# WKV-7 recurrence: all four head pairs in one step, a written order on all compute engines, a triangular inverse by blocks of 16

## The chip, the cores and the metric

The kernel runs on one core of a Trainium2 chip. A core has TensorE (PE in the views; PEld is its weight load), VectorE (DVE), ScalarE (ACT), GpSimd (POOL) and SyncE (SP, which issues DMAs here). Each engine works through its own queue in order; semaphores tie the queues together. The metric is the device time of one execution in microseconds, as the median of several runs.

## The reference

One layer of a hybrid encoder block on 1024 positions with a model width of 1024, all in float32. After a norm and one input projection, branch A is latent attention with 8 heads, branch B the bidirectional WKV-7 recurrence with 8 heads of 64, and both are gated, merged and added to the input. A gated feed-forward part with a depthwise convolution follows.

```python
h = rms_norm(x)
proj = h @ w_in
o_a = mla_branch(...)                  # 8 heads, softmax over all positions
o_b = rwkv7_branch(...)                # see below
y = sig(gA) * (o_a @ w_o[:512]) + sig(gB) * (o_b @ w_o[512:])
x = x + y @ w_merge
x = x + (silu(dwconv(rms_norm(x) @ w_gate)) * (rms_norm(x) @ w_up)) @ w_down

def step(state, inp):                  # one position of one head, 64 x 64 state
    r_t, w_t, k_t, v_t, a_t, b_t = inp
    sa = einsum('bhvk,bhk->bhv', state, a_t)
    state = state * w_t + sa[..., None] * b_t + v_t[..., None] * k_t
    return state, einsum('bhvk,bhk->bhv', state, r_t)
# run once forward and once backward; then a norm per head, a bonus term and a gate
```

## The kernel before

**Stages.** Up to about 340 us the kernel projects the columns of both branches (`weave`). From there to about 1278 us runs a mixed stage, which the change rebuilds. Branch B's output product and the merge follow, to 1390 us, and then the feed-forward part with blocked products (L1591, L1684 to L1686), to the end. The change leaves the feed-forward part as it is.

**The dense stream of the mixed stage.** `dense()` hands out products in small pieces: `gates()` (16 tiles of gate columns, L254, L255, L257), `attention()` (8 heads of 16 steps) and `branch0()` (branch A's output product). A precise product is three matmuls: high part by high part, low by high and high by low; `split` makes the two parts with a cast on ACT (L168, `whi` from the loaded weights `wraw`) and a subtraction on POOL or DVE (L169, `wlo`). An attention step is three score matmuls (L1214 to L1216), the exponential on ACT (L123), a cast (`ph`, L1225), its low part (`pl`, L1226, POOL) and three products with the values (L1188 to L1190). `maxima` (L1158 to L1165) finds each row's largest score ahead of a head.

**The recurrence.** It is worked in chunks of 64 positions. A unit is one head pair and one half of the sequence, in both directions, 8 chunks; there are 8 units. `prep_a` makes for a unit the matrix `NM` (L798) and the inverse of each chunk's triangular 64 x 64 matrix: the two 32 x 32 blocks on its diagonal go through memory (`dn`, read back as `IN`) into a layout with one block a partition, and DVE eliminates them in 31 steps of a multiplication into `tm` (L819) and an addition into `Ti` (L823). The result goes through memory again in two layouts (`dT`, `dU`, read back as `TT` and `U`, L841 and L843), and two sets of matmuls (L852, L863) fill in the block beside the diagonal. `prep_b` makes the operands `Er` (L904), `Ek` (L915) and `BT` (L928).

**The chain.** `chain` then takes a unit's chunks one after the other. A chunk has three hops that wait for each other: L980 (the state `RR` times `Ek`, copied to `rh` on ACT), L992 (times the inverse `TT`, copied to `RR` by DVE and ACT, L993 and L994) and L1005 (times `BT`; on DVE, L1010, the product `sm` of the old state with the chunk's decay, which POOL has made at L988, is added). L952 sets the values into the next `RR`, and `chunk_out` (L961, L966) makes the output, which `gnorm` (L1034, L1044) normalises and gates. Each matmul set of a hop is four matmuls: two directions, two heads.

**What sets the order.** In the mixed stage only TensorE's instructions stand in the order in which the program writes them; DVE, ACT and POOL are ordered by a scheduler. The program writes them with a planner: its loop keeps a clock `now`, advances it by each dense piece, and emits a hop when the table `LATENCY` says that its inputs are there, a preparation step (`prepare`) when it is due, and else a dense piece (`fill`). `DENSE` is the dense work between two hops. In the feed-forward part all engines and SP stand in written order.

Of the kernel before, what the change touches and what calls it, by code (L numbers as in the profile page):

```python
# [25 lines left out]
NPAIR = 4  # L26
DECAY = math.exp(-0.5)
# [19 lines left out]
LAG = 3  # L47

LATENCY = {
    "a0": 4000, "a1": 5000, "a2": 4000, "a3": 4000, "nm": 2100, "nz": 7020, "inv": 32000, "u": 10000, "y": 2125, "t": 2500,  # L50
    "b0": 5600, "b1": 0, "b2": 3720, "er": 2400, "ak": 2160, "sb": 4900, "bt": 1500, "hop": 1000, "gn": 4500, "last": 1500,
}
AHEAD = 6
DENSE = (920, 1000, 1000, 1150, 1070, 1150, 1150, 1150)
CARRY = 1000
# [10 lines left out]
HOPC = 450  # L66
PREPC = 0.8
# [20 lines left out]
def block_kernel(ctx: ExitStack, tc: tile.TileContext, a):  # L88
    nc = tc.nc
    V, S, G = nc.vector, nc.scalar, nc.gpsimd  # L90
# [16 lines left out]
    cur = {"set": None, "load": None, "group": []}  # L107

# [37 lines left out]
    def dt(name, shape):  # L146
# [4 lines left out]
    d_rw = {q: [dt(f"d_{q}{p}", [128, T]) for p in range(NPAIR)]  # L151
            for q in ("r", "v", "kk", "x1", "x2", "s0", "s1", "bo")}
# [8 lines left out]
    d_oa, d_ob = ([[dt(f"d_o{b}{x}{p}", [128, T]) for x in "hl"] for p in range(NPAIR)] for b in "ab")  # L161
# [217 lines left out]

    def inproj(j, done):  # L380
        ps = big()
        for k in range(8):
            if k % 4 == 0:
                wh, wl = wcols(a["w_in"][j], k // 4)
            ws = slice(k % 4 * 128, (k % 4 + 1) * 128)
            mmk(ps, wh[:, ws], wl[:, ws], hx[k], k == 0, k == 7)
            if k == 7:
                done(ps)
            yield 1280
# [27 lines left out]

    now = [0.0]
# [153 lines left out]
    def rw_done(p, q):  # L572
        def done(ps):
            t = keep(q, "rkv"[q] + "t")
            shift(ps, 4 + 4 * q + p, t)
            if q != 1:
                nc.sync.dma_start(d_rw["rkv"[q]][p], t)
            rkv[p, q] = t
        return done

    def rw_prep(p):
# [4 lines left out]
        for dst, wt, src, bias, key in (  # L586
# [11 lines left out]
            if key:  # L598
                nc.sync.dma_start(d_rw[key][p], dst)
# [8 lines left out]
        for h in range(2):  # L608
            nc.sync.dma_start(d_rw[("x2", "x1")[h]][p][H[h], :], kf[H[h], :])
# [7 lines left out]
        nc.sync.dma_start(d_rw["kk"][p], nr)  # L617
        V.scalar_tensor_tensor(out=at, in0=at, scalar=-1.0, in1=nr, op0=mult, op1=mult)
        for h in range(2):
            nc.sync.dma_start(d_rw[("x1", "x2")[h]][p][H[h], :], at[H[h], :])  # L620
# [12 lines left out]
        nc.sync.dma_start(d_rw["bo"][p], bo)  # L633

    def gate_done(j):
        def done(ps):
            for x, hs in zip(ps, HT):
                gt = wpool["g"].tile([128, 512], F32, tag="gt", name="gt")
                V.tensor_tensor(out=gt, in0=x, in1=rstd[:, hs], op=mult)
                (S if j >= 14 else nc.sync).dma_start(d_gate[j][:, hs], gt)  # L640
# [56 lines left out]
    for p in range(NPAIR):  # L697
        weave(*[inproj(T_RKV + 3 * p + q, rw_done(p, q)) for q in (1, 0, 2)])
    parts(True)
# [5 lines left out]
    G.memset(smask.rearrange("p (c t) -> p c t", t=C)[:, :, 0:1], 0.0)  # L705
    TTt = [cbp.tile([128, NCH, C], F32, name=f"TT{d}") for d in range(2)]
# [3 lines left out]

    wpool["g"] = ctx.enter_context(pool("gp", side="right"))
    sb = ExitStack()
# [6 lines left out]

    def scb():  # L720
        return pw.tile([128, 512], F32, tag="sc", name="sc", bufs=SC_BUFS)

    def ctb():
        return pw.tile([128, 2, C], F32, tag="ct", name="ct", bufs=CT_BUFS)
# [7 lines left out]

    def half(src):
        t = wk.tile([128, 512], F32, tag="ld", name="ld", bufs=4)
        nc.sync.dma_start(t, src)
# [3 lines left out]
    def dirs(d, t):  # L739
        return (t if d == 0 else t[:, ::-1]).rearrange("p (f c t) -> p f c t", c=4, t=C)  # L740
# [4 lines left out]
    def after(key, i):  # L745

        if key in state:
            tc.add_manual_dep(i.ins, state[key].ins.name, NOSYNC, reason="after the recurrence's step")

    def prep_a(p, w, n, q):  # L750

        hts = (HT[w], HT[1 - w])
# [5 lines left out]
        sg = [half(d_rw[f"s{d}"][p][:, hts[d]]) for d in range(2)]  # L758
        x1 = [half(d_rw["x1"][p][:, hts[d]]) for d in range(2)]
        yield "a0", 0  # L760

        for d in range(2):
            t = sg[d] if d == 0 else sg[d][:, ::-1]
            after("dve", V.tensor_tensor_scan(t, smask, t, 0.0, mult, add))
            after("act", act(of(d, pin), dirs(d, sg[d]), AF.Exp, scale=-DECAY))
            act(of(d, iP), dirs(d, sg[d]), AF.Exp, scale=DECAY)
        pcs = wk.tile([128, NCH], F32, tag="pcs", name="pcs", bufs=3)
        wk.tile([128, 16], F32, tag="pad2", name="pad")
        V.tensor_copy(pcs[:, :, None], last)
        q.update(pin=pin, pcs=pcs)  # L770
        kk = [half(d_rw["kk"][p][:, hts[d]]) for d in range(2)]
        yield "a1", 0

        BK = [wk.tile([128, 8, 128], F32, tag="BK", name="BK", bufs=3) for _ in range(2)]
        AXk = [wk.tile([128, 8, C], F32, tag="AXk", name="AXk", bufs=3) for _ in range(2)]

        def times(eng, key, dst, src, f, cs):
            for hf in range(2):
                for d in range(2):
                    after(key, eng.tensor_tensor(out=dst[hf][:, 4 * d:4 * d + 4, cs], in0=dirs(d, src[d])[:, hf],  # L780
                                                 in1=of(d, f)[:, hf], op=mult))

        times(G, "pool", BK, x1, iP, H[0])
        times(V, "dve", AXk, kk, pex, H[0])
        x2 = [half(d_rw["x2"][p][:, hts[d]]) for d in range(2)]
        q.update(BK=BK, AXk=AXk)
        yield "a2", 0

        times(G, "pool", BK, x2, iP, H[1])
        yield "a3", 0  # L790

        NM = take("NM", n, [128, NCH, C])
        for c0_ in (0, 8):
# [6 lines left out]
            if c0_ == 0:  # L800
                yield "nm", 1300
        dn = dr.tile([2, 2, NCH, 32, 32], F32, tag="dn", name="dn", bufs=2)
        for h in range(2):
            for b in range(2):
                r0 = h * 64 + b * 32
                nc.sync.dma_start(dn[h, b].rearrange("c s t -> s c t"), NM[r0:r0 + 32, :, b * 32:b * 32 + 32])
        IN = take("IN", n, [128, 32, 32])
        for i in range(4):
            nc.sync.dma_start(IN[32 * i:32 * i + 32], dn[i // 2, i % 2][None].to_broadcast([2, NCH, 32, 32]))
        yield "nz", 1300  # L810

        Ti = wk.tile([128, 32, 16], F32, tag="Ti", name="Ti")
        G.memset(Ti, 0.0)
        for i in range(2):
            V.tensor_copy(Ti.rearrange("p t j -> p (t j)")[:, 16 * i:16 * i + 496:33], cst[:, C_TI + i:C_TI + i + 1].to_broadcast([128, 16]))
        for s in range(31):
            nt, nj = 31 - s, s // 2 + 1
            tm = wk.tile([128, 32, 16], F32, tag="tm", name="tm")
            t = V.tensor_tensor(out=tm[:, 0:nt, 0:nj], in0=IN[:, s, s + 1:32][:, :, None].to_broadcast([128, nt, nj]),  # L819
                            in1=Ti[:, s, 0:nj][:, None, :].to_broadcast([128, nt, nj]), op=mult)  # L820
            if s == 0:
                after("dve", t)
            V.tensor_tensor(out=Ti[:, s + 1:32, 0:nj], in0=Ti[:, s + 1:32, 0:nj], in1=tm[:, 0:nt, 0:nj], op=add)  # L823
        Tq = wk.tile([128, 16, 32], F32, tag="tm", name="Tq")
        S.copy(Tq, Ti.rearrange("p t j -> p j t"))
        dT = dr.tile([2, 2, 16, 2 * NCH, 32], F32, tag="dT", name="dT", bufs=2)
        dU = dr.tile([2, 32, 2 * NCH, 16], F32, tag="dU", name="dU", bufs=2)
        for h in range(2):
# [1184 lines left out]
```

## Time and profile before

| what | us |
|---|---|
| median of 3 runs (2094.4 to 2099.11) | 2096.95 |
| the profiled execution | 2094.12 |
| its span, by the profile | 2092.3 |

A row of a window gives, for a stretch from A to B, its length and each engine's busy time with the number of its instructions, then the clock that TensorE was granted as a share of full speed, the DMA engines' busy share and the bytes moved a second. A row of waits names the waiting engine, the tile and line it waits in, then what ended the wait, with the total, the number and the longest in us. A row of instructions by line gives busy time and the mean of one in ns, and behind the next bar the idle time ahead of them with what ended it. An fp32 matmul is worked in two passes and leaves two records.

### The profile page before, as it was taken

To read this page: it belongs to the slowest core of one execution; us is meant where nothing else is said; L and a number is where in the kernel's file an instruction comes from. 1 tells how busy PE (TensorE), PEld (TensorE's weight loads), DVE (VectorE), ACT (ScalarE), POOL (GpSimd) and SP (SyncE) were. 2 spreads that over 40 slices of the span, in tenths; PEclk is the share of its full clock that TensorE was granted. 3 is DMA by queue.
4 is the path that set the end of the run, shared out by engine and by line. 5 is a ranking of instruction groups with operands and counts; after the bars stand their busy time and mean duration, and the time that the engine had idled before them with its cause. 6 is when DMAs were issued, how large, how long until landed. Compare 5 with 4: busy or idle time off the path is not lost.

```text
span 2092.3 us, 31850 instructions
## 1 busy us (share of the span) xinstructions
PE 1900.7 (91%) x12016; PEld 1462.3 (70%) x12016; DVE 1316.8 (63%) x2112; ACT 912.6 (44%) x1603; POOL 821.1 (39%) x718
## 2 busy tenths in 40 slices
PE   7799999799898887788788999998999999999998
PEld 5566667676666565566556677876788888888887
DVE  7566666636383957585957134458767666766677
ACT  4676564123233454565556753444233233322331
POOL 7344546232223565555546632223522222222221
PEclk9999999899999888998989999999999999999999
DMA  3147446452436153434433378210111111111112
GB/s 146 34 142 229 141 163 205 124 142 75 137 95 174 43 141 99 94 99 114 108 88 94 102 272 298 94 57 30 51 61 46 61 46 61 46 61 45 61 47 100
DMA packets 216714, 221.09 MB, mean 106 GB/s; under 512 B 113960, under 2 KB 145768, under 8 KB 216560
## 3 DMA queue, kind: packets, MB, share of 16 engines
q1 hardware_dynamic: 215984, 218.01, 34.5%
q8 instruction: 94, 1.54, 0.3%
q10 hardware_dynamic: 576, 1.05, 0.1%
q14 instruction: 60, 0.49, 0.1%
HBM read 151.20 MB, written 63.60 MB: 103 GB/s over the span
## 4 chain that ended last, share of the span: by engine, by line
PE 44%; DVE 11%; DMA 4%; issue 2%; ACT 1%; SPq 1%; POOL 0%; DVEq 0%; ACTq 0%; POOLq 0%
PE b L1591 18%; PE b L1685 4%; PE b L1686 3%; PE b L1684 3%; DMA IN<-dn 2%; DVE Ti L823 2%; PE b L257 2%; PE b L254 2%; PE b L255 2%; DVE tm L819 2%; DVE mx L1159 1%; PE po L1188 1%; PE st L1214 1%; PE st L1215 1%; PE st L1216 1%
## 5 line engine op out<-in xcount | busy, mean ns | idle before, releaser
L169 POOL TENSOR_TENSOR wlo<-wraw,whi 128x512 fp32r<-128x512 f32 x118 | 161.8, 1372 | 512.3 <-ACT whi L168 506.6
L1226 POOL TENSOR_TENSOR pl<-pe,ph 128x512 fp32r<-128x512 f32 x128 | 169.8, 1329 | 131.5 <-ACT ph L1225 129.1
L254 PE MATMUL st<-hh,whi 128*128 128x512 f32 x408 | 176.4, 432 | 16.7 <-ACT hh L281 9.0
L255 PE MATMUL st<-hl,whi 128*128 128x512 f32 x408 | 165.2, 405 | 0.5 <-DVE hl L282 0.5
L1696 DVE TENSOR_TENSOR x<-b,x 128x512 f32<-128x512 f32 x176 | 119.2, 687 | 54.7 <-PE b L1686 54.7
L819 DVE TENSOR_TENSOR tm<-IN,Ti 128x126 f32<-128x126 f32 (+22 forms) x248 | 95.1, 383 | 80.2 <-DMA IN<-dn 74.0
L257 PE MATMUL st<-hh,wlo 128*128 128x512 f32 x408 | 141.5, 402 | 1.3 <-POOL wlo L169 1.3
L168 ACT CAST whi<-wraw 128x512 fp32r<-128x512 f32 x118 | 72.9, 619 | 142.2 <-PE po L255 35.2
L254 PEld LDWEIGHTS st<-hh,whi 128*128 128x128 f32 x408 | 79.8, 196 | 46.2 <-issue 11.1
L1225 ACT CAST ph<-pe 128x512 fp32r<-128x512 f32 x128 | 79.1, 620 | 65.3 <-PE po L1190 63.3
L823 DVE TENSOR_TENSOR Ti<-Ti,tm 128x126 f32<-128x126 f32 (+22 forms) x248 | 101.0, 407 | 6.6
L988 POOL TENSOR_TENSOR sm<-RR,pcs 64x128 f32<-64x128 f32 x112 | 47.5, 424 | 145.0 <-DVE RR L1010 108.6
L169 POOL TENSOR_TENSOR wl<-wraw,wh 128x512 fp32r<-128x512 f32 x22 | 28.9, 1313 | 179.7 <-ACT wh L168 179.7
L123 ACT ACTIVATE pe<-st 128x512 f32<-128x512 f32 x128 | 76.3, 597 | 39.9 <-PE st L1216 33.3
L257 PEld LDWEIGHTS st<-hh,wlo 128*128 128x128 f32 x408 | 79.3, 195 | 20.2 <-POOL wlo L169 2.2
L255 PEld LDWEIGHTS st<-hl,whi 128*128 128x128 f32 x408 | 80.0, 196 | 16.4 <-issue 1.2
L1159 DVE TENSOR_REDUCE mx<-st 128x1 f32<-128x512 f32 x112 | 73.3, 683 | 28.3 <-PE st L1158 28.0
L954 ACT COPY RR<-sc 64x256 f32<-64x256 f32 x128 | 47.0, 367 | 57.6 <-PE sc L952 53.2
L1684 PE MATMUL b<-sh,wh 128*128 128x512 f32 x176 | 69.1, 393 | 2.7 <-ACT sh L1640 2.7
L1685 PE MATMUL b<-sl,wh 128*128 128x512 f32 x176 | 69.3, 394 | 0.8 <-DVE sl L1649 0.8
L1684 PE MATMUL b<-sh,whi 128*128 128x512 f32 x176 | 68.6, 390 | 1.3 <-DVE x L1696 1.3
L1686 PE MATMUL b<-sh,wl 128*128 128x512 f32 x176 | 69.2, 393 | 0.0
(502 smaller groups left out, 5529.3 us busy)
## 6 DMA issues: line engine op xcount, KB each, us to landing
wraw<-w_in SPq DMA_DIRECT2D x64, 256.0 KB
wraw<-w_fd SPq DMA_DIRECT2D x44, 256.0 KB
AA<-w_fu SPq DMA_DIRECT2D x41, 256.0 KB
A<-w_fg SPq DMA_DIRECT2D x41, 256.0 KB
ld<-d_x SPq DMA_DIRECT2D x32, 256.0 KB
d_gate<-gt SPq DMA_DIRECT2D x28, 256.0 KB
xt<-xT SPq DMA_DIRECT2D x8, 512.0 KB
d_s<-sg SPq DMA_DIRECT2D x8, 512.0 KB
```

Source lines behind the costliest of these rows:

```text
L169: (eng or G).tensor_tensor(out=lo, in0=x, in1=hi.bitcast(F32), op=sub)
L254: nc.tensor.matmul(o, wh, xh[:, hs], start=first, stop=False)
L255: nc.tensor.matmul(o, wh, xl[:, hs], start=False, stop=False)
L257: nc.tensor.matmul(o, wl, xh[:, hs], start=False, stop=last)
L819: t = V.tensor_tensor(out=tm[:, 0:nt, 0:nj], in0=IN[:, s, s + 1:32][:, :, None].to_broadcast([128, nt, nj]), in1=Ti[:, s, 0:nj][:, None, : ...
L823: V.tensor_tensor(out=Ti[:, s + 1:32, 0:nj], in0=Ti[:, s + 1:32, 0:nj], in1=tm[:, 0:nt, 0:nj], op=add)
L1226: G.tensor_tensor(out=pl, in0=pe, in1=ph.bitcast(F32), op=sub)
L1591: nc.tensor.matmul(b, wt[:, ws], x, start=(first and k == 0 and m == 0), stop=(k == 3 and m == 2), skip_group_check=True)
L1684: nc.tensor.matmul(b, wh[:, ws], xh[:, hs], start=(k == 0), stop=False)
L1685: nc.tensor.matmul(b, wh[:, ws], xl[:, hs], start=False, stop=False)
L1686: nc.tensor.matmul(b, wl[:, ws], xh[:, hs], start=False, stop=(k == 1))
L1696: V.tensor_tensor(out=x2[j][:, hs], in0=b, in1=x2[j][:, hs], op=add)
```

## The change

The diff has 1303 lines. A unit is now 128 positions in each direction of all four head pairs: 8 units of 2 chunks. So `chain(n, q, osb)` has 16 steps instead of 64, and each matmul set runs over `EACH`, 8 slots of direction and pair, for two heads: 16 matmuls, with one evacuation. `RR` is two tiles, one for each head of a pair. The product with the decay moves from the operands and from `sm` onto the state itself: an addition on DVE and then a multiplication with `pcs` on POOL for one head and on DVE for the other.

The inverse is worked in blocks of 16: DVE eliminates in 15 steps, and the blocks beside the diagonal are filled in by matmuls in two levels, with products `P`, `X`, `PY`, `Y` and `TT`. `NM`'s blocks go to memory in 8 writes and return in one read; the inverse goes out in two writes and returns in 14 reads of 16 x 16 blocks (`Un` and `TT`).

DVE, ACT and POOL stand in written order in the mixed stage too. `Clocked` wraps each engine and keeps a planned clock of it, from a fixed cost and one for each element; the planner's loop reads these clocks instead of `LATENCY`. Rows of instructions that go through it name its line, L104. The four banks of PSUM with the tag `sc` are shared by the chain, the preparation and the maxima.

In attention every other step makes two exponentials on ACT (`ph` and, in place, the full value) and its low part on DVE; the other steps do as before. Weights of the gates and of branch A are loaded ahead through a queue (`queue`, `prefetch`, `weights`). `gnorm` works in pieces of 128 columns and keeps three of the four pairs' results in SBUF instead of writing them to memory. After the mixed stage the first two tiles of branch B's product are interleaved (`mixture`), and `x2` is loaded behind all of them.

```diff
-LAG = 3
-LATENCY = {
-    "a0": 4000, "a1": 5000, "a2": 4000, "a3": 4000, "nm": 2100, "nz": 7020, "inv": 32000, "u": 10000, "y": 2125, "t": 2500,
...
+LAG = 4
+DENSE = (1500,) * 8
+SLACK = 1500
+MARGIN = 300
+BACKLOG = 4000
+HOP = 300
+CARRY = 3000
...
+    V, S, G = Clocked(nc.vector, 140, 1.04), Clocked(nc.scalar, 140, 0.92), Clocked(nc.gpsimd, 100, 2.35)
...
+    written.enter_context(tc.manual_schedule(engines={getattr(mybir.EngineType, n) for n in ("PE", "DVE", "Activation", "Pool")}))
+    ordered(True)
...
-        for s in range(31):
-            nt, nj = 31 - s, s // 2 + 1
+        for s in range(15):
+            nt, nj = 15 - s, s + 1
...
+        for g in range(8):
+            rows, b = slice(16 * g, 16 * g + 16), g % 4
+            if b != 3:
+                nc.sync.dma_start(Un[rows, :, b % 2 * 16:b % 2 * 16 + 16], dU[g].rearrange("c t j -> t c j"))
+            nc.sync.dma_start(TT[rows, :, b * 16:b * 16 + 16], dT[g].rearrange("c j t -> j c t"))
...
+        for c, r, b in each4:
+            nc.tensor.matmul(p3[r:r + 32, c], NM[r:r + 16, c, b:b + 32], Un[r:r + 16, c, 0:16], start=True, stop=True)
+        S.activation(P, p3, AF.Copy, scale=cst[:, C_TI + 1:C_TI + 2])
...
-            for d in range(2):
+            for s, d, c in EACH:
                 for h, hs in enumerate(H):
-                    nc.tensor.matmul(ct[hs, d, :], BT[:, d, i % 4, hs], RR[:, d, h, 1, :], start=(d == 0), stop=(d == 1))
+                    nc.tensor.matmul(ct[hs, s, :], BT[:, d, c, hs], RR[h][:, s, 1, :], start=(s == 0), stop=(s == 7))
             for h, hs in enumerate(H):
...
-                    V.tensor_tensor(out=nxt[hs, :, h, 0, :], in0=ct[hs], in1=sm[hs], op=add)
+                    V.tensor_tensor(out=z, in0=ct[hs], in1=RR[h][hs, :, 0, :], op=add)
+                    (G if h == 0 else V).tensor_tensor(out=z, in0=z, in1=pc, op=mult)
...
-        for k in range(26):
+        for k in range(9):
...
-            now += HOPC
-            ready = now + LATENCY["hop"]
+            now[0] += x
+            ready = max(now[0], ends[0] + x) + HOP
```

The first place is in attention, on TensorE, around hops of the chain. Of before, with `st` the scores, `po` the products with the values and `ct` the chain's:

```order
L980 MATMUL ct<-RR,Ek 64x64 x4
L961 MATMUL ct<-Er,RR 64x64 x4
L966 MATMUL ct<-AXr_2707,RR 64x64 x4
L1214 MATMUL st<-qh_2721,kh_2722 128x512
L1215 MATMUL st<-ql,kh_2722 128x512
L1216 MATMUL st<-qh_2721,kl 128x512
L1158 MATMUL st<-kh_5988,qh_5987 128x512 x2
L992 MATMUL ct<-rh,TT_2691 64x64 x4
L952 MATMUL sc<-cst,vv 64x64 x4
L1188 MATMUL po<-ph,vhh_5989 128x512
```

Of the changed kernel at a like place (L1289 to L1291 are the scores, L1247 to L1249 the products with the values, L1217 the maxima, L858 the preparation's `NM`, L1055 the hop with the inverse):

```order
L858 MATMUL sc<-AXk,BK 64x64 x16
L1247 MATMUL po<-ph,vhh_6917 128x512
L1248 MATMUL po<-pl,vhh_6917 128x512
L1249 MATMUL po<-ph,vhl_6919 128x512
L1289 MATMUL st<-qh_2701,kh_2702 128x512
L1290 MATMUL st<-ql,kh_2702 128x512
L1291 MATMUL st<-qh_2701,kl 128x512
L1217 MATMUL sc<-kh_6915,qh_6914 128x512 x2
L1055 MATMUL ct<-rh,TT_2671 64x64 x16
L1247 MATMUL po<-ph,vhh_6916 128x512
```

Three matmul sets of four stand with one attention step between them and the next hop; now a set of sixteen (L1055, which was L992) stands with a whole step and the maxima ahead of it.

The second place is on DVE in attention, where the elimination, the maxima (`mx`) and the chain's copies meet. Of before:

```order
L823 TENSOR_TENSOR Ti<-Ti,tm 128x12x10
L1159 TENSOR_REDUCE mx_8592<-st 128x1
L819 TENSOR_TENSOR tm<-IN,Ti 128x11x11
L1159 TENSOR_REDUCE mx_8592<-st 128x1
L993 COPY RR<-ct 64x2x64
L823 TENSOR_TENSOR Ti<-Ti,tm 128x11x11
L819 TENSOR_TENSOR tm<-IN,Ti 128x10x11
L823 TENSOR_TENSOR Ti<-Ti,tm 128x10x11
L1159 TENSOR_REDUCE mx_8592<-st 128x1
L819 TENSOR_TENSOR tm<-IN,Ti 128x9x12
L1159 TENSOR_REDUCE mx_8592<-st 128x1
L1010 TENSOR_TENSOR RR<-ct,sm 64x2x64 x2
```

Of the changed kernel:

```order
L104 COPY RR_7464<-ct 64x8x64
L104 TENSOR_REDUCE mx_8580<-sc 128x1 x2
L104 TENSOR_TENSOR pl<-st,ph 128x512
L104 TENSOR_REDUCE mx_8580<-sc 128x1 x2
L104 TENSOR_TENSOR RR_8606<-ct,RR_7464 64x8x64
L104 TENSOR_TENSOR RR_8607<-ct,RR_7465 64x8x64
L104 TENSOR_TENSOR RR_8607<-RR_8607,pcs 64x8x64
L104 TENSOR_TENSOR tm<-IN,Ti 128x15
L104 TENSOR_TENSOR Ti<-Ti,tm 128x15
L104 TENSOR_TENSOR tm<-IN,Ti 128x14x2
L104 TENSOR_TENSOR Ti<-Ti,tm 128x14x2
L104 TENSOR_REDUCE mx_8580<-sc 128x1 x2
```

The elimination's operations went from 32 x 32 blocks to ones that fit 16 x 16, the chain's copies from 64x2x64 to 64x8x64, and low parts of the softmax (`pl`) and the product with `pcs` joined the queue.

The third place is ACT's queue in the gate part, where the casts of weights stand among the chain's copies. Of before:

```order
L929 COPY BT<-sc 128x512
L168 CAST whi<-wraw 128x512
L982 COPY rh<-ct 128x128
L929 COPY BT<-sc 128x512
L954 COPY RR<-sc 64x2x128
L994 COPY RR<-ct 64x2x64
L954 COPY RR<-sc 64x2x128
L982 COPY rh<-ct 128x128
L967 COPY osb<-ct 128x2x64
L954 COPY RR<-sc 64x2x128 x2
L994 COPY RR<-ct 64x2x64
L168 CAST whi<-wraw 128x512
```

Of the changed kernel:

```order
L104 COPY BT<-sc 128x512
L104 CAST whi<-wraw 128x512
L104 COPY rh<-ct 128x512
L104 COPY RR_3651<-ct 64x8x64
L104 COPY RR_3744<-sc 64x1024
L104 COPY RR_3745<-sc 64x1024
L104 CAST whi<-wraw 128x512
L104 COPY rh<-ct 128x512
L104 COPY osb<-ct 128x8x64
L104 COPY RR_3745<-ct 64x8x64
L104 CAST whi<-wraw 128x512
```

A cast that waits for its weights stands ahead of `rh` and `RR` in both; the order is now the one in which the program writes them.

More of the change, by code (lines that the diff above doesn't have):

```diff
@@ L377, in block_kernel, with prefetch, weights @@
         V.tensor_scalar(gqs[:, i:i + 1], vc(n), 1.0 / math.sqrt(96.0), None, op0=mult)
+    queue, ahead, hold = [], [], []
+    def prefetch():
+        if queue:
+            ahead.append(queue.pop(0)())
+    def weights():
+        if not ahead:
+            prefetch()
+        return ahead.pop(0)
     def inproj(j, done):
@@ L784, in prep_a, with times @@
[L784 to L790, printed above, removed]
+        AXk = [wk.tile([128, 8, C], F32, tag="AXk", name="AXk", bufs=2) for _ in range(2)]
+        def times(eng, dst, src, f, cs, i):
+            hf, d = i // 2, i % 2
+            eng.tensor_tensor(out=dst[hf][:, 4 * d:4 * d + 4, cs], in0=dirs(d, src[d])[:, hf], in1=of(d, f)[:, hf], op=mult)
```

693 lines of the change are left out of this document (389 added, 304 removed).

## The prediction

> **What bounds the kernel now.** I read the table of busy engines first, then the span cut into stages, then what TensorE waits for in the stage that the change rebuilds.
>
> ```profile
> PE 1900.7 (91%) x12016; PEld 1462.3 (70%) x12016; DVE 1316.8 (63%) x2112; ACT 912.6 (44%) x1603; POOL 821.1 (39%) x718
> PE 44%; DVE 11%; DMA 4%; issue 2%; ACT 1%; SPq 1%; POOL 0%; DVEq 0%; ACTq 0%; POOLq 0%
> core 0: us, PE busy (x) PEld busy (x) DVE busy (x) ACT busy (x) POOL busy (x), PEclk, DMA share, GB/s
> 340.00:1278.00 938.00, 806.19 (x7429) 594.18 (x7428) 552.55 (x1169) 423.87 (x894) 422.36 (x442) 0.93 0.46 127
> 455.00:660.00 205.00, 188.64 (x1946) 140.40 (x1945) 114.81 (x283) 59.10 (x148) 58.18 (x77) 0.96 0.44 116
> 660.00:1140.00 480.00, 388.09 (x3741) 278.40 (x3740) 337.55 (x689) 259.02 (x551) 253.26 (x254) 0.89 0.39 99
> 1140.00:1255.00 115.00, 112.02 (x1015) 80.30 (x1015) 31.05 (x64) 76.68 (x150) 62.00 (x61) 1.00 0.54 181
> 1480.00:2092.30 612.30, 603.57 (x2662) 499.13 (x2660) 413.39 (x581) 185.53 (x274) 160.54 (x121) 1.00 0.17 57
> ```
>
> TensorE bounds the kernel: 91% busy, with 44% of the chain that ended last. The change rebuilds the stage from 340 to 1278 us, in which attention, gate products and the recurrence share the engines. There TensorE is busy for 806.19 of 938 us, so **131.8 us are idle**, and its granted clock is 0.93. From 660 to 1140 us (81% busy) the clock is 0.89; where TensorE is 97% busy (1140 to 1255) it is 1.00. No other engine comes near the stage's length (DVE 552.55, ACT 423.87, POOL 422.36). The last stage, whose engines all run in written order already, is 98.6% busy at 1.00 and isn't touched. TensorE's waits from 340 to 1260 us (total, times, longest) say where the idle time is, and one row from 1255 to 1290 tells the end of the stage:
>
> ```profile
> PE ct L980 <- DVE RR L1010: 36.7, 8, 9.0
> PE st L1158 <- DVE mx L1159: 12.3, 7, 4.4
> PE ct L1005 <- DVE RR L993: 9.2, 6, 2.7
> PE sc L904 <- DVE tm L819: 9.1, 1, 9.1
> PE st L1165 <- DVE mx L1162: 7.8, 4, 2.6
> ...
> PE sc L904 <- DVE Er L905: 5.3, 1, 5.3
> ...
> PE st L1214 <- DVE mx L1159: 4.1, 4, 1.8
> ...
> PE b L254 <- ACT whi L168: 5.0, 1, 5.0
> ```
>
> The chain of the recurrence (L980, L1005) takes 45.9 us of it, nearly all because DVE is late with the chain's small tiles; the maxima (L1158, L1165, L1214) 24.2; the preparation (L904) 14.4; the end 5.0. That names 89.5 of the 131.8 us. The other 42 are many small rows.
>
> **The change, part by part.** The sum is made against the profiled execution (2094.1 us, span 2092.3); the median of the runs, 2096.95, is 2.8 above it, and I add that at the end.
>
> *Term 1, chain bursts.* The chain's matmuls keep their number, but 16 run in a row instead of 4: 376 bursts (64 steps of L980, L992, L952 and L961, 60 of L1005 and L966) become 94. The price of a burst is the time from its start to the next start:
>
> ```profile
> 692.60 0.45 PE L980 MATMUL ct<-RR,Ek 128*64 128x64 f32 x8
> 692.88 0.40 PE L961 MATMUL ct<-Er,RR 128*64 128x64 f32 x8
> 693.22 0.45 PE L966 MATMUL ct<-AXr,RR 64*64 64x64 f32 x8
> 693.59 0.50 PE L1214 MATMUL st<-qh,kh 128*128 128x512 f32 x1
> 694.94 0.45 PE L992 MATMUL ct<-rh,TT 64*64 64x64 f32 x8
> 695.32 0.45 PE L952 MATMUL sc<-cst,vv 128*64 128x64 f32 x8
> 695.70 0.50 PE L1188 MATMUL po<-ph,vhh 128*128 128x512 f32 x1
> ```
>
> The chain of waits has whole sets of 16, 32 and 8 matmuls with their durations:
>
> ```profile
> 768.80 1.08 PE sc L798 x32
> 956.72 1.13 PE sc L852 x64
> 1137.98 1.78 PE sc L904 x16
> ```
>
> An fp32 matmul leaves two records, so x8 is a burst of four. The starts lie 0.28, 0.34, 0.37, 0.38 and 0.38 us apart, mean 0.35: 376 × 0.35 = 131.6 us. Sixteen matmuls of the same width (64 columns, L798 in the chain of waits) took 1.08 us, so 94 × 1.08 = 101.5 us: **−30**. At the cheapest gap of four, 0.28, it would be −4; at the dearest, 0.38, −41.
>
> *Term 2, Er.* 128 matmuls of 128 columns (L904, 8 in 1.78 us, 0.222 each: 28.5 us) become 256 with 64 rows and 64 columns, at the 0.0675 of L798 17.3 us: **−11**. If L904's row was stretched by its waits and its true price is near twice 0.0675, there is nothing to gain: 0 to −13.
>
> *Term 3, the inverse by blocks of 16.* On TensorE 512 products of 32 columns (L852 and L863, 32 in 1.13 us, 0.0353 each, 18.1 us) become 256 of 32 columns and 1792 of 16. No row shows 16 columns. From 64 to 32 columns the price halves (0.0675 to 0.0353), so I halve it once more: 256 × 0.0353 + 1792 × 0.0177 = 40.7 us, **+23**. The other end is no saving below 32 columns: 2048 × 0.0353 = 72.3, +54. I take the low end because the halving is what the nearest two rows show.
>
> The Trainium skill speaks against this part: "TensorEngine Tiling (Array Packing)", section Instruction Overhead, gives each matmul some 60 cycles of overhead, says that one column lasts as long as 60, and advises against cutting a dimension that is small already. The trace does not agree at 32 columns, which cost half of 64 (0.0353 against 0.0675); no row shows 16. By the page this term would be the +54, a rival below.
>
> What DVE gains by the smaller blocks is large:
>
> ```profile
> L823 DVE TENSOR_TENSOR Ti<-Ti,tm 128x126 f32<-128x126 f32 (+22 forms) x248 | 101.0, 407 | 6.6
> L819 DVE TENSOR_TENSOR tm<-IN,Ti 128x126 f32<-128x126 f32 (+22 forms) x248 | 95.1, 383 | 80.2 <-DMA IN<-dn 74.0
> L905 DVE TENSOR_TENSOR Er<-sc,cst 128x512 f32<-128x512 f32 x32 | 21.6, 686 | 8.9 <-PE sc L904 8.7
> L1226 POOL TENSOR_TENSOR pl<-pe,ph 128x512 fp32r<-128x512 f32 x128 | 169.8, 1329 | 131.5 <-ACT ph L1225 129.1
> L988 POOL TENSOR_TENSOR sm<-RR,pcs 64x128 f32<-64x128 f32 x112 | 47.5, 424 | 145.0 <-DVE RR L1010 108.6 <-DVE RR L1008 23.0 <-ACT ph L1225 9.3
> ```
>
> The 496 elimination operations (196 us) become 240 of at most 64 elements a row; at no more than the mean of 395 ns that is under 95 us, so DVE loses over 100. It gains half of the low parts of the softmax (64 of 128; 64 × 0.686 from L905 = 44 us), and POOL loses their 64 × 1.329 = 85 us and the 47.5 of L988. Both stay far under the stage's length, so this enters only through the waits. ACT does two exponentials in half of the steps and has larger copies; with 424 of 938 us busy, attention's products hide that.
>
> *Term 4, TensorE's idle time.* The chain waited 45.9 us over 376 bursts; with a quarter as many hops, and 6 to 24 dense matmuls written between any two of them, I let a quarter stay: −35. The hops get longer: the state's update is now an addition of 512 elements a row on DVE, near 0.69 us by L905, and then, for one head of each pair, the product with the decay on POOL, near 1.33 by L1226. The dense matmuls written there hide it; without them 15 updates would cost 15 × 2.02 = 30 us. The one wait of L904 on the elimination and that on Er go with the shorter elimination: −15. Of the maxima a third goes, since DVE is freed: −8. The end of the stage −5, since the weights are now fetched ahead. Of the 42 us of small rows half: −20. Together −83.
>
> A new wait comes with it. The block-wise copies of the inverse return through memory in 14 small reads where 6 stood (four of L841, two of L843):
>
> ```profile
> 848.63 1.29 SPq L841 DMA_DIRECT2D TT<-dT  x2
> 849.98 0.61 SPq L843 DMA_DIRECT2D U<-dU  x1
> ```
>
> Ahead of them, writes and the read of IN fall from 14 to 11, so SP has five more issues in each of 8 units, at 0.61 us 24 us in all. But the 14 stand in one lump of 8.5 us: the loads of queries, keys and the next unit stand behind them on SP, and TensorE's first products on the blocks, with the dense matmuls behind those, wait for the last. I let about half of the 24 reach TensorE, +13. **Term 4 is −70.** Its ends: −132 if no idle time stays, and about −10 if the old waits are merely replaced.
>
> *Term 5, the clock.* At 0.93 the stage's 806 busy us lose 7%, about 57 us. With terms 1 to 4 TensorE would be busy for some 92% of the stage, as it is from 455 to 660 us, where the clock was 0.96: about 762 × 0.04 = 30 us lost. **−27**, between 0 and −57.
>
> Sum: −30 − 11 + 23 − 70 − 27 = **−115**, so 1979 for the profiled execution and **1982 us** as a median. What else is edited costs nothing here: the weight queue, the merged mixture and the norm's pieces move loads whose transfers lie beside products, and the stage after 1390 us keeps its code. If that cover is gone, it is the wait rival below.
>
> **The rivals.** *Sixteen columns cost as much as 32*, since a product has a least price that the rows down to 32 columns don't show: term 3 is +54, 31 us more, 2013. For it: the finest cut is the change's own; against it: the halving just above. This is what the page named under term 3 says of narrow products.
>
> *All idle time goes.* The last stage, in written order, is 98.6% busy at a clock of 1.00. If the mixed stage comes near that, term 4 is −115 and term 5 −57: sum −190, 1907. For it: DVE, ACT and POOL are all under 60% there. Against it: the chain is serial, and the last stage has none.
>
> *New DMA waits.* The chain needs each unit's inverse. All 14 reads issued late cost 14 × 0.61 = 8.5 us a unit, 68 in 8 units; instead of +13, and with the clock where it is: −30 − 11 + 23 − 83 + 68 = −33, 2064. For it: a load of 16 x 16 blocks was never timed here, and the elimination waited 74 us for the like before:
>
> ```profile
> DVE tm L819 <- DMA IN<-dn: 74.0, 8, 13.4
> ACT rh L982 <- PE ct L980: 83.6, 36, 9.8
> ACT whi L168 <- DMA wraw<-w_in: 12.3, 2, 11.5
> ```
>
> Against it: units stand one attention stretch apart, so that a read has 823 / 8, some 100 us.
>
> *Slower: a written queue on ACT is blocked.* In the gate part a cast of weights now stands, in written order, ahead of the chain's copy of `rh` or `RR`; if its weights come late, the chain stops, and TensorE, also in written order, stops with it. The row above shows two such waits, 12.3 us, mean 6.1. Thirty-two half tiles of gate weights at 6 us each would be 192 us, −115 + 192 = +77: 2174. It decides from 115 / 32 = 3.6 us each. Against it: the weights are fetched ahead of use, and only two waits showed in the old order.
>
> **How the numbers follow.** Chances: forecast 0.46 (own range 1945 to 2030), 16 columns at the price of 32 0.08, all idle time gone 0.20, DMA waits 0.15, blocked queue 0.11. The range 1890 to 2080 takes in all but the blocked queue and the far ends of its neighbours. Anything within 0.2% (4.2 us, about what a measurement of this kernel can tell from no change) could only be the end of the DMA case, 0.03 of its 0.15; the rest of it is faster. So faster 0.86, same 0.03, slower 0.11.
>
> **What would show it.** Term 1: a burst of 16 at 1.0 to 1.1 us, 94 of them. Term 2: Er's matmuls at 0.07 us. Term 3: the products of 16 columns at 0.018 or at 0.035 us each. Term 4: TensorE idle for 50 to 75 us from the first gate product to the start of the merge; a row of TensorE on the copies TT or Un would be the DMA case, one of ACT's casts on `wraw` with the chain behind them the blocked queue. Term 5: a clock near 0.96. It would be wrong as a whole if DVE, in written order, turned out late for the maxima and the chain at once: then TensorE's rows on DVE would stay at 60 us or more.

## The result, and the profile after

| | before | changed |
|---|---|---|
| median of 4 runs | 2095.68 | **1984.44** (1979.03 to 1988.33) |
| profiled execution, span | 2094.12, 2092.3 | 1986.8, 1985.0 |

The ratio is 0.9473 (95% interval 0.9435 to 0.9512). The forecast was 1982 us as a median, by taking 115 us off the profiled execution; that execution and its span lost 107.3. The page's table of busy engines, of the changed kernel:

```profile
PE 1859.7 (94%) x15440; PEld 1484.7 (75%) x15440; DVE 1224.6 (62%) x1837; ACT 870.5 (44%) x1378; POOL 652.9 (33%) x550
```

The windows' columns are those of the prediction. A fair cut of the mixed stage ends at the first product of branch B (tile `b` from `o`, in the changed kernel `obh`), at 1261.1 us before and 1159.0 now; its start, 340 us, is the same work in both (1155 and 1150 rows of TensorE ahead of it). The two stretches around that cut, of before:

```profile
340.00:1261.10 921.10, 794.26 (x7380) 584.57 (x7379) 545.22 (x1160) 417.76 (x888) 419.83 (x440) 0.93 0.45 123
1261.10:1312.80 51.70, 46.47 (x194) 37.46 (x192) 28.58 (x29) 20.07 (x23) 12.11 (x9) 0.93 0.89 315
```

And of the changed kernel, to the end:

```profile
340.00:1159.00 819.00, 756.76 (x10809) 609.00 (x10808) 452.10 (x886) 372.18 (x660) 253.26 (x272) 0.94 0.48 127
1159.00:1202.50 43.50, 43.50 (x193) 36.03 (x192) 25.33 (x26) 17.57 (x21) 11.62 (x8) 1.00 0.72 242
1202.50:1299.80 97.30, 91.13 (x385) 74.27 (x384) 48.34 (x67) 44.34 (x77) 23.59 (x18) 0.96 0.30 110
1299.80:1985.00 685.20, 663.90 (x2909) 546.32 (x2907) 475.83 (x653) 218.18 (x325) 191.80 (x138) 0.99 0.16 55
```

The mixed stage lost 102.1 us: TensorE's idle time went from 126.8 to 62.2 us (length less busy), its busy time from 794.3 to 756.8. Branch B's product lost 8.2, of which 5.2 was idle; what follows took 3 us more. TensorE's waits in the stage (total, times, longest) are almost all new ones:

```profile
PE po L1247 <- ACT rc L104: 17.6, 10, 4.3
PE sc L914 <- issue: 11.2, 4, 3.8
PE st L278 <- ACT whi L104: 8.8, 2, 8.6
PE sc L901 <- DMA Un<-dU: 8.2, 7, 1.9
PE ct L1046 <- DVE mx L104: 4.9, 3, 2.9
PE sc L926 <- issue: 3.0, 1, 3.0
PE sc L907 <- issue: 2.2, 3, 1.0
PE sc L1224 <- DVE mx L104: 1.6, 1, 1.6
```

The chain's 45.9 us are down to the 4.9 of L1046, the preparation's 14.4 are gone, and of the maxima's 24.2 the 1.6 of L1224 stay. All of TensorE's rows on DVE together went from 97 us (340 to 1261) to 6.5. In their place stand the logarithm of the softmax's sums (`rc`, 17.6), gaps inside the narrow products that nothing in the profile releases ("issue", 16.4 in three rows), one late cast of weights, and the reads of `Un`.

Where the busy time went comes from the start times of all TensorE rows of the stage, each row counted to the start of the next, without idle time; a cut by rows like that isn't stretched by the modelled ends:

| rows | before | changed |
|---|---|---|
| chain (six matmul sets) | 149.7 | 99.7 |
| dense stream | 521.6 | 490.8 |
| inverse | 18.5 | 60.2 |
| `Er` | 33.8 | 32.7 |
| norm | 21.7 | 26.0 |
| other preparation | 48.9 | 47.5 |

### The profile page after: what moved, and what is told of

The parts are those of the page before. It is cut to its first block, busy times and chain, and to the rows that moved or that the text cites. A ratio compares the mean times of both kernels' runs of the same rounds, so it can differ in the third digit from the quotient of the medians.

```text
span 1985.0 us, 37748 instructions
## 1 busy us (share of the span) xinstructions
PE 1859.7 (94%) x15440; PEld 1484.7 (75%) x15440; DVE 1224.6 (62%) x1837; ACT 870.5 (44%) x1378; POOL 652.9 (33%) x550
## 5 line engine op out<-in xcount | busy, mean ns | idle before, releaser
L104 POOL TENSOR_TENSOR wlo<-wraw,whi 128x512 fp32r<-128x512 f32 x118 | 161.0, 1365 | 633.0 <-ACT whi L104 613.0
L104 DVE TENSOR_TENSOR x<-b,x 128x512 f32<-128x512 f32 x176 | 119.2, 686 | 54.6 <-PE b L1817 54.6
L104 POOL TENSOR_TENSOR pl<-pe,ph 128x512 fp32r<-128x512 f32 x64 | 84.3, 1316 | 207.5 <-ACT ph L104 188.8
L104 ACT CAST whi<-wraw 128x512 fp32r<-128x512 f32 x118 | 72.7, 618 | 104.6 <-PE po L279 29.0
L279 PEld LDWEIGHTS st<-hl,whi 128*128 128x128 f32 x408 | 80.3, 197 | 17.6 <-DVE hl L104 1.7
L104 DVE TENSOR_REDUCE mx<-sc 128x1 f32<-128x512 f32 x128 | 81.7, 681 | 12.3 <-PE sc L1217 11.9
L104 POOL TENSOR_TENSOR wl<-wraw,wh 128x512 fp32r<-128x512 f32 x22 | 28.9, 1314 | 179.5 <-ACT wh L104 169.7
L1247 PE MATMUL po<-ph,vhh 128*128 128x512 f32 x128 | 58.9, 460 | 17.6 <-ACT rc L104 17.6
L104 DVE TENSOR_TENSOR u<-b,p 128x512 f32<-128x512 f32 x42 | 29.0, 691 | 72.0 <-PE b L1722 69.4
L1816 PE MATMUL b<-sl,whi 128*128 128x512 f32 x176 | 68.5, 389 | 0.0
L1817 PE MATMUL b<-sh,wlo 128*128 128x512 f32 x176 | 68.5, 389 | 0.0
L104 ACT CAST whi<-s 128x512 fp32r<-128x512 f32 x33 | 20.5, 622 | 89.7 <-PE b L1816 44.0
L1289 PE MATMUL st<-qh,kh 128*128 128x512 f32 x128 | 59.2, 462 | 0.0
```

The source lines that it names most:

```text
L104: return f(*args, **kw)
L279: nc.tensor.matmul(o, wh, xl[:, hs], start=False, stop=False)
L1247: nc.tensor.matmul(po[0], vhk, ph, start=(kt == 0), stop=False)
L1289: nc.tensor.matmul(ps, kh[:, ks], qh[:, qs], start=True, stop=False)
L1816: nc.tensor.matmul(b, wh[:, ws], xl[:, hs], start=False, stop=False)
L1817: nc.tensor.matmul(b, wl[:, ws], xh[:, hs], start=False, stop=(k == 1))
```

## The experiments

The questions were which part of the change took the time off, and what its terms cost. No run makes the steps small again (64 of them in place of 16) with all else as changed, so what the larger steps give by themselves stays argued. All times are medians, to be read against 2090 to 2096 us before and 1984.44 us as changed.

### One part undone, with the planner left to itself

**The inverse by blocks of 32 again** (e1). Elimination, transfers and products as before, in the changed kernel:

```diff
-        for s in range(15):
-            nt, nj = 15 - s, s + 1
+        for s in range(31):
+            nt, nj = 31 - s, s // 2 + 1
...
-    A_STEPS = (..., ("inv", 15, V), ("tq", 1, S), ("u", 1, None), ("p", 1, S), ("x", 1, V), ("y", 1, V), ...)
+    A_STEPS = (..., ("inv", 31, V), ("tq", 1, S), ("u", 1, None), ("y", 1, V), ...)
```

> The changed kernel with the inverse of before: blocks of 32, 31 elimination steps on DVE, two sets of products of 32 columns, six reads of TT and U. Theory (the blocks of 16 cost more than they give): TensorE's inverse products fall from 60 to about 19 us of the mixed stage, its gaps with no releaser inside those products (16 us) go, DVE gains about 100 us that the stage has room for: 1925 to 1945 us. Rival (the blocks of 16 pay, since the long elimination on DVE was what held the chain and the maxima back): TensorE's waits on DVE come back by more than 40 us, 1985 to 2020 us.

2095.71 us (ratio 1.0021, 1.0009 to 1.0034): the whole gain is gone, beyond what either theory had. The windows before and behind the last score product of attention, at 973 us:

```profile
640.00:975.00 335.00, 286.69 (x2516) 223.73 (x2515) 222.22 (x419) 201.86 (x359) 116.76 (x101) 0.95 0.40 99
975.00:1258.50 283.50, 183.87 (x2637) 152.34 (x2635) 144.33 (x346) 95.11 (x163) 58.82 (x78) 0.77 0.43 115
```

The second row tells why: for 283.5 us the chain ran on with attention used up, TensorE 65% busy at a clock of 0.77. In the trace the first and the last operation of a unit's elimination lay up to 116 us apart (up to 53 in the kernel before), since the planner had spread them.

**The same with the elimination in four runs** (e6):

```diff
-            yield 0, None if s < 30 else 500
+            if s % 8 == 6:
+                yield 0, None if s < 30 else 500
```

> The kernel of e1 (inverse by blocks of 32) with the elimination's 31 steps written in four runs of seven to eight instead of one at a time between other steps. Theory (a unit's elimination takes about 100 us in e1 because the planner writes its 62 DVE operations apart, so the units fall behind the dense stream, which ends 250 us before the chain): an elimination of 25 to 45 us, the dense stream lasts, 1950 to 1985 us. Rival (the 196 us of DVE work itself is too much for this stage, however it is placed): 2040 us or more, with TensorE's waits on DVE over 60 us.

2056.26 us. The elimination did get shorter (24 to 72 us a unit), and 40 us came back, but not the rest: the rival's time, though TensorE's rows on DVE are 41 us and not the 60 that it gave. These two runs can't say whether DVE's work or the planner's new order costs it.

**DVE, ACT and POOL back to the scheduler** (e2), TensorE's order as changed:

```diff
-    written.enter_context(tc.manual_schedule(engines={... ("PE", "DVE", "Activation", "Pool")}))
-    ordered(True)
```

> The changed kernel with DVE, ACT and POOL ordered by the scheduler again in the mixed stage; TensorE's order, steps and sizes as changed. Theory (written order took most of the 65 us of idle time): TensorE's idle time in the mixed stage goes from 62 back to 100 to 125 us, 2020 to 2055 us. Rival (the larger steps alone took it, a quarter of the hops): idle time stays within 15 us of 62, 1975 to 2000 us.

2004.75 us. Of its mixed stage the window reads:

```profile
340.00:1174.40 834.40, 762.38 (x10807) 612.62 (x10806) 437.57 (x887) 372.15 (x659) 251.04 (x272) 0.94 0.47 124
```

72.0 us are idle, 10 more than in written order, which is the rival's size and not the theory's; the time lies between the two ranges. Written order on the three engines is worth about 20 of the 111 us; the rest comes with the steps, the smaller blocks and the plan.

**Every attention step with one exponential and its low part on POOL** (e5):

```diff
-                    if npl[0] % 2:
+                    if False:
```

> The changed kernel with every attention step as before: one exponential and a cast on ACT, the low part on POOL. Theory (POOL has room, 253 of 819 us, and the low part is wanted a step later): within 8 us of the changed kernel. Rival (the low part on DVE, 0.69 in place of 1.33 us, keeps the products from waiting): waits of TensorE on POOL's pl of 15 us or more, 2000 us or more.

2006.1 us, slower as the rival said, but not through its wait: TensorE's row on POOL's `pl` is 2.5 us. TensorE waited for loads that had come nearly in time in the changed kernel (1.1 us there; rows of this kernel, in the stage):

```profile
PE sc L1217 <- DMA qh<-d_qrh: 10.9, 4, 5.7
...
PE po L1248 <- POOL pl L104: 2.5, 4, 1.6
```

The planner's clocks of the engines had moved, and with them the whole order, so what the split itself is worth stays open.

**A dense piece after every fourth matmul of a burst** (e4):

```diff
             for s, d, c in EACH:
                 ...
+                if s in (1, 3, 5):
+                    fill()
```

> The changed kernel with a piece of the dense stream written into each burst of sixteen after every fourth matmul, so that the chain is in bursts of four again with the same evacuations. Theory (a burst of four costs 0.40 us and not a quarter of 1.06, and the dense matmul at a switch 0.08 more): some 280 more breaks at 0.2 us, TensorE busy 50 to 60 us more in the mixed stage, 2035 to 2045 us. Rival (the chain got cheaper because TensorE waits less at half clock, not because of the bursts): busy time within 15 us, 1985 to 2000 us.

2135.61 us, with TensorE 92 us busier; but attention was used up at 1032 us and the chain ended at 1290, so that much of it is the end of e1 over again. The experiment was too strong to price a burst.

### Three single mends, planned anew

The products `Y` in one set (e7), the first unit's scan planned later (e8), and the softmax's sums copied out by DVE (e9):

```diff
-                nc.tensor.matmul(p3[ib, c, 0:16], NM[ia, c, 32:64], U[ia, c], start=True, stop=True)
-                nc.tensor.matmul(p3[ib, c, 16:32], NM[ia, c, 32:64], Un[ia, c, 16:32], start=True, stop=True)
+                nc.tensor.matmul(p3[ib, c], NM[ia, c, 32:64], U[ia, c], start=True, stop=True)
...
-        yield 0, 3000
+        yield 0, 3000 if n else 12000
...
-                act(rc[own], po[0][oth], AF.Ln)
+                V.tensor_copy(rc[own], po[0][oth])
```

> The changed kernel with the 512 products Y of 16 columns made as 256 of 32 columns; POOL copies 32 x 256 elements beside it. Theory (a narrow product costs by its number in its quarter of the array, not by its columns): the products Y fall from 17.4 to about 9.5 us, and gaps with no releaser there get fewer, 1971 to 1981 us. Rival (the cost goes by columns): Y stays at 16 to 18 us, 1982 to 1988 us.

> The changed kernel with the first unit's scan planned 12 us behind its loads and not 3. Theory (the wait of 8.6 us at 355 us is ACT's written queue: a cast of weights stands behind the exponentials of a scan that waits for its load): the wait goes, 1974 to 1980 us. Rival (the first unit's chain is what counts, and starts later for it): 1984 us or more.

> The changed kernel with the softmax's sums copied out of PSUM by DVE, and the logarithm made later from there. Theory (the 17.6 us in front of the first product of a head half come from ACT's written queue, in which the logarithm stands behind copies that wait for DVE): that row falls below 6 us, 1970 to 1978 us. Rival (DVE's queue is as late as ACT's, and gains 11 us of work): the row turns into one on DVE of the same size, 1982 to 1992 us.

1991.95, 1996.38 and 2032.75 us: none faster than the changed kernel. In e7 the products `Y` fell from 17.4 to 9.2 us, as the theory had it, and in e8 the wait at 355 us went; yet both lost it elsewhere, in other waits and behind the mixed stage. In e9 the rival's row came, though the time is 40 us beyond its range, and the wait only changed its name:

```profile
PE po L1247 <- DVE rc L104: 16.4, 10, 4.4
```

A planner that reads engine clocks answers every edit with a new order for all that follows. So the planner's choices of the changed kernel were written down as a list and replayed. The list was not run without an edit; in the trace of r3, below, whose two edits are small, the order on TensorE, DVE and ACT is the changed kernel's except at the edits, and on SP a few transfers change places.

### The same edits in the replayed order

**Blocks of 32 in the changed kernel's order** (r1): two or three elimination steps where one stood, the steps `P` and `X` empty.

```diff
-                t = max([ready] + [seen.get(x, math.inf) for x in want])
-                ...
-                x = prepare(thin or sparse and t < math.inf)
+                x = plan.pop(0)
...
+            if s % 2 and s < 29 or s == 30:
+                yield 0, None if s < 30 else 500
```

> From here on the planner's choices of the changed kernel (which piece of dense work, preparation step or hop comes next) are written down as a list and replayed, so that an edit moves nothing else. This kernel: the inverse by blocks of 32 in that list, two or three elimination steps where one stood, the steps P and X empty. Theory (blocks of 16 pay because a unit's elimination ends in time in queues that are worked in written order; one that ends some 10 us late holds up ACT's copy Tq and all behind it, in 8 units): TensorE's idle time in the mixed stage 120 us or more, 2020 to 2080 us, though its busy time falls by 30 to 40 us. Rival (e1 and e6 lost only by the planner's new order, and DVE has room for the longer elimination): idle time under 80 us, 1945 to 1985 us.

2042.69 us, the theory's time. The window of its mixed stage, then its waits of TensorE and of ACT:

```profile
340.00:1215.10 875.10, 737.54 (x7736) 588.26 (x7735) 522.15 (x1134) 366.99 (x644) 256.36 (x263) 0.91 0.48 126
```

```profile
PE po L1252 <- ACT rc L121: 32.8, 12, 4.1
PE ct L1051 <- DVE mx L121: 22.8, 3, 8.0
PE ct L1071 <- DVE RR L121: 18.3, 2, 9.6
...
ACT RR L121 <- DVE RR L121: 80.1, 14, 15.8
...
ACT Tq L121 <- DVE Ti L121: 34.2, 4, 19.4
```

In the changed kernel the last two rows read:

```profile
ACT RR L104 <- DVE RR L104: 38.8, 14, 5.9
...
ACT Tq L104 <- DVE Ti L104: 12.4, 4, 5.0
```

DVE is busy only 70 us longer (522 against 452, in a stage of 875), but its queue is late at the places that others wait for: ACT stands up to 19.4 us in front of the copy `Tq`, and TensorE is idle for 137.6 us in place of 62.2. Its rows on DVE are 67 us in place of 6.5. Its busy time falls by only 19 us, though the inverse takes 21.2 us in place of 60.2, as the clock falls too (0.91). So the blocks of 16 cost TensorE about 40 us of products, and in this order the kernel is 58 us slower without them. An order made for the longer elimination could do better; e6, the one that the planner made, was slower still.

**Bursts broken after every fourth matmul, as far as dense pieces stood behind** (r2): 126 breaks, so 220 bursts for 94, with one dense piece left behind each hop.

```diff
+    def apart():
+        k = plan.index("h") if "h" in plan else 0
+        if plan[:k].count("f") > 1:
+            plan.remove("f")
+            fill()
```

> The replayed list, with dense pieces that stood behind a hop written into its bursts after every fourth matmul, one piece being left behind each hop: 220 bursts in place of 94, all else in place. Theory (each break costs about 0.2 us: a burst of four 0.40 us in place of a quarter of 1.06, and the dense matmul at a switch 0.08 more): 126 breaks, TensorE busy 20 to 30 us more in the mixed stage. Rival (bursts don't matter, the chain was dear before because of the half clock): busy time within 8 us. Some idle time may come on top, since less dense work lies between hops: 2000 to 2040 us by the theory, 1985 to 2010 by the rival.

2059.92 us. The window of the mixed stage, then two sets of the chain by line, with busy time and ns of one behind the first bar:

```profile
340.00:1234.20 894.20, 820.19 (x10811) 624.61 (x10811) 450.54 (x886) 373.21 (x660) 251.93 (x273) 0.93 0.44 116
```

```profile
L1093 PE MATMUL ct<-RR,BT 128*64 128x64 f32 x480 | 24.9, 231 | 0.5 <-ACT RR L121 0.5
L1080 PE MATMUL ct<-rh,TT 64*64 64x64 f32 x512 | 23.1, 227 | 1.7 <-ACT rh L121 1.7
```

The same two sets in bursts of sixteen, in the changed kernel:

```profile
L1055 PE MATMUL ct<-rh,TT 64*64 64x64 f32 x512 | 18.4, 221 | 0.0
...
L1066 PE MATMUL ct<-RR,BT 128*64 128x64 f32 x480 | 17.9, 230 | 0.0
```

One matmul's duration is nearly the same (227 for 221 ns, 231 for 230); what is lost at a break is the overlap of one with the next. The chain's six sets went from 99.7 to 125.2 us, 0.20 us a break, and the dense stream, the same products, from 490.8 to 520: TensorE was busy 63 us more with 12 us more idle. The theory's sign and cause, at twice its size, and a time beyond its range. Part of the excess is clock (0.93 in place of 0.94, some 8 of the 63 us if busy time goes with it); why it fell wasn't settled.

**The two mends in the replayed order** (r3): `Y` in one set, and four pieces of gate products ahead of the first unit's scan.

```diff
-PLAN = """0 fx3 0x2 fx2 0x2 fx4 ...
+PLAN = """0 fx7 0x2 fx2 0x2 ...
```

> The replayed list with two edits: the 512 products Y of 16 columns as 256 of 32 columns, and four pieces of gate products ahead of the first unit's scan and exponentials. Theory (e7 and e8 each took its wait or price away, and lost it again by the planner's new order): Y at 9 us in place of 17, the wait of 8.6 us at 355 us gone, 1965 to 1976 us. Rival (the time comes back at the next late thing whatever the order): 1981 to 1988 us.

**1964.03 us** (ratio 0.9383, 0.9358 to 0.9408), faster than both kernels. Its waits of TensorE in the mixed stage:

```profile
PE po L1264 <- ACT rc L121: 17.3, 10, 4.3
...
PE st L295 <- ACT whi L121: 2.9, 2, 2.6
```

The late cast went from 8.8 to 2.9 us. A whole set of `Y` in the changed kernel's timeline, 128 records from the first to the next product, and then in this kernel:

```profile
510.32 0.24 PE L925 MATMUL sc<-U,NM 32*32 32x16 f32 x4
...
512.31 0.24 PE L926 MATMUL sc<-Un,NM 32*32 32x16 f32 x4
512.47 0.50 PE L278 MATMUL st<-hh,whi 128*128 128x512 f32 x1
```

```profile
494.67 1.20 PE L943 MATMUL sc<-U,NM 32*32 32x32 f32 x64
495.80 0.50 PE L295 MATMUL st<-hh,whi 128*128 128x512 f32 x1
```

2.15 us became 1.13: 16.8 ns a record of 16 columns, 17.7 of 32.

**Both halves behind the inverse copied by ACT** (r4), on r3:

```diff
-            V.tensor_copy(RR[0][H[0], :, 1, :], ct[H[0]])
+            S.copy(RR[0][H[0], :, 1, :], ct[H[0]])
```

> The kernel of r3, with both halves of the hop behind the inverse copied by ACT (they were shared by DVE and ACT, and ACT's copy waited for DVE's, 38.8 us in all in the changed kernel). Theory (ACT's queue in written order passes DVE's lateness on to the softmax's logarithm and so to TensorE, the 17.6 us ahead of L1247): that row falls below 9 us, 1955 to 1966 us. Rival (ACT gains 10 us of work and the hop gets longer): no change to slower than r3, 1968 to 1985 us.

1975.3 us, slower than r3. ACT no longer waits for DVE's `RR`, but the row of TensorE on `rc` stays:

```profile
PE po L1264 <- ACT rc L121: 17.9, 10, 4.3
```

```profile
ACT rc L121 <- DVE pv L121: 24.4, 13, 4.5
```

What the logarithm waits for is DVE's copy `pv` out of the same bank, not ACT's queue; the theory of e9 and r4 was wrong there. In the longest such wait of the changed kernel the last product of a head half ended at 875.79 us, `pv` started at 879.41, behind maxima in DVE's queue, and `rc` started at 880.14, 0.03 us behind the end of `pv`. A kernel that takes `pv` off DVE wasn't tried.

## Why the prediction was right

The sum came within 8 us of the span's change (−115 against −107.3). Its main claim held: TensorE's idle time in the mixed stage, above all that behind DVE, was the largest thing to gain, and its rows on DVE did not stay at the 60 us that would have shown the whole to be wrong. But only the total of that largest term was right, and the others missed both ways, so that the closeness of the sum is in good part luck. The median came nearer still, within 2.4 us, by chance: the profiled execution lies 2.4 above the median of the changed kernel, where the forecast had put it 2.8 below.

Measured, the change adds up so: the chain −50, the dense stream −31, the inverse +42, `Er` and the other preparation −2, the norm +4, idle time −70, branch B's busy time −3, what follows +3, together −107.

- **Term 1, −30: −50.** A burst of sixteen takes the 1.08 us that was read (99.7 / 94 = 1.06). The price of four was mis-sized: 149.7 / 376 = 0.40 us over the stage in place of the 0.35 of the five gaps that were quoted. Those five lay in a stretch at a clock of 1.00, and the stage had 0.93. r2 shows the breaks as the cause.
- **Term 2, −11: −1.** The step that failed is the price, 0.0675 from L798. `Er`'s products took 32.7 / 256 = 0.128 us, and the end of the range with no gain came out. Their row by line:

```profile
L973 PE MATMUL sc<-AXr,BK 64*128 64x64 f32 x512 | 33.7, 284 | 0.0
```

  They fill 64 rows by 128 columns of the array (64\*128), L798's a quarter of it (64\*64), of which the code puts two side by side; so the cheap price was that of two at once. The chain's sets of 128 rows by 64 columns (L1066, 16.1 / 240 = 0.067) have the cheap price too, so it seems to be the columns that count. This is read from the shapes, and no run varied it.
- **Term 3, +23: +42.** The halving from 64 to 32 columns did not go on to 16 in the sets that the code puts on two of the array's four row groups (`Y`, 17.4 / 512 = 0.034 a product, as dear as 32 columns); the sets on all four, `P` and `PY`, took 13.0 / 512 = 0.025 and 0.021. The rival with one price for 16 and 32 columns was nearer for `X` and `Y`. The Trainium skill, "TensorEngine Tiling (Array Packing)", section Instruction Overhead, is borne out as far as r3 goes: below 32 columns the number of products counts, not their width. Its figure of 60 columns is not, as a price from one start to the next, since 32 cost half of 64. The section speaks of latency, though, and the prediction held a price against it: the profile's durations of one record differ less, 191 ns for 32 columns (L852) and 218 for 64 (L798).
- **Term 4, −70: −70** (126.8 + 5.2 idle against 62.2), but through parts that missed both ways: the old waits gave 120 us for 83, the new ones took 51 for 13. Its parts: the chain −41 for −35, the preparation −14 for −15, the maxima −23 for −8, the end −5 for −5; the small rows −37 for −20. The new wait on the blocks' reads was 8.2 for 13. Not foreseen were `rc` (17.6) and the gaps in the narrow products (16.4). A blocked queue on ACT, as in the rival, did come once (8.6 us), but the other way round: the cast at 363 us didn't hold others up for its weights, it stood behind exponentials whose scan on DVE waited for its load (first ACT's rows, then DVE's and TensorE's):

```profile
361.03 0.63 ACT L104 ACTIVATE Pp<-ld 128x512 f32<-128x512 f32 x1 [9.01 <-DVE ld L104]
...
363.16 1.12 ACT L104 CAST whi<-wraw 128x512 fp32r<-128x512 f32 x2
...
359.73 2.34 DVE L104 TENSOR_TENSOR_SCAN ld<-smask,ld 128x512 f32<-128x512 f32 x2 [8.94 <-DMA ld<-d_s]
...
363.81 0.80 PE L278 MATMUL st<-hh,whi 128*128 128x512 f32 x1 [8.56 <-ACT whi L104]
```

- **Term 5, −27 for the clock: −12 by the same working**, since the clock rose to 0.94 and not to 0.96 (757 × 0.06 = 45 us lost, for 57). The dense stream got cheaper by 31 us all the same. r2 made it 29 us dearer with the same products, some 5 of them by its clock (0.93 for 0.94), and so shows that breaks can be much of that: a part of term 1 that was left out, on the dense side of each switch. At r2's rate the 282 breaks that the change saves would give over 50 us and not 31, so that this account stays open.
- The norm's smaller pieces cost 4 us that no term had.
- Where the prediction let DVE's shorter elimination enter "only through the waits", that was the point on which all hung. The elimination took 65 us of DVE's time for 196, and r1, with the longer one back, has 75 us more idle time on TensorE.

## What to carry to other kernels

Read a matmul's price from a row of the same shape, as far as the array's rows and columns that it fills go, and from a whole stage rather than from a few gaps; count the switches between streams on both sides. In queues that are worked in written order an engine that is half idle can still be the bound, by being late at one place: ask what stands behind each step, not how busy its engine is. And where a planner sets the order, replay its list when one edit is to be measured, or the edit's effect drowns in the new order.

## What the runs showed of the hardware that was not expected

Long sets of narrow matmuls seem to have outrun TensorE's supply of instructions. In the middle of a set of `PY` TensorE stopped, with no releaser in the profile (the timeline of the changed kernel):

```profile
500.76 1.14 PE L914 MATMUL sc<-TT,P 32*16 32x16 f32 x96
505.69 0.40 PE L914 MATMUL sc<-TT,P 32*16 32x16 f32 x28 [3.79 <-issue]
```

The DMA view of just that gap has one packet, of 16 KB, on an instruction queue (packets, MB, share):

```profile
q8 instruction: 1, 0.02, 1.6%
```

In the four such gaps of `PY` (2.0 to 3.8 us) the work went on 1.2 to 1.6 us after such a packet had landed, and in the four of r3 1.2 to 1.4 us after one. In r1, which has none of the sets `X` and `PY`, TensorE has no row with "issue" at all. That the supply of instructions is the cause is argued from these times, not tried by itself.
